# Expert stage of a two-layer encoder: evictions queued one chunk behind their matmuls, one-hots two chunks ahead, splits of 2048 columns with four chunks of room and seven raw buffers

## The chip, the cores and the metric

One core of a Trainium2 chip runs the whole kernel. The metric is device time in microseconds (us), taken as the median of several runs. The profile is one execution, recorded by the hardware profiler; its engines are PE (TensorE matmuls; PEld are its weight loads), DVE (VectorE), ACT (ScalarE), POOL (GpSimd) and SP (SyncE, which here issues the weight loads from HBM).

## What is computed

Two layers of a post-norm encoder trunk on 256 tokens of width 1024. Layer 1 ends in a dense SwiGLU, layer 2 in a top-2-of-8 expert SwiGLU:

```
logits = x @ w_router + b_router
gates  = softmax over the top 2 of 8, zero elsewhere
out    = sum over e of gates[:, e] * ((silu(x @ w1[e]) * (x @ w3[e])) @ w2[e])
x      = LayerNorm(alpha * x + out + ple)
```

Each expert has w1 and w3 of 1024 x 3584 and w2 of 3584 x 1024, all float32: 352 MB for the eight, and every byte is read once. The change touches only this expert stage, which in the kernel before runs from about 685 us to 1620 us of the span.

## The kernel before

**Accuracy scheme.** PE multiplies in float32r. To keep float32 accuracy, every operand is split in two: `hi` is the value rounded to float32r (a copy on ACT, line 95), `lo` is the value minus `hi` (a subtraction on DVE, line 96). A product then takes three matmuls: hi.hi, hi.lo, lo.hi (`mm3`, lines 253 to 255). So every weight that arrives is read once by ACT and once by DVE before PE can use it.

**Chunks.** The expert weights come as 336 chunks of 1 MB, each a tile of 128 x 2048 floats. SP loads chunk g into a raw buffer; there are nine, in the order of `MOE_RAW` (the tags misc, Q, Q, act, act, raw x4). `prepare` splits it as two halves of 1024 columns, each into one `hl` tile that holds hi and lo of the half; there is room for six halves (`MOE_HL`), that is for three chunks. `prepare` runs four halves ahead of the half that PE multiplies (`MOE_LEAD = 4`). A raw buffer is loaded again once the second half's subtraction has read it; a room is written again once PE has multiplied the half in it.

**Experts and blocks.** A routing step orders the experts by their number of tokens. The first four are *heavy* (128 slots), the last four *light* (64 slots, where hi and lo of the tokens lie side by side in the 128 columns, so that two matmuls do instead of three, lines 1216 and 1217). Each expert's 3584 hidden columns are cut in blocks of 1024, 1024, 1024 and 512. From the third block on, light and heavy blocks alternate. For block i the program goes through w1 (`kind` 0), half of the second multiplication (w2, `down`) of block i-1, w3 (`kind` 1), and the other half of that `down`: twelve chunks for a full block.

**Small work between chunks.** After a part, `gated` takes its results out of PSUM (silu or copy on ACT, a product on DVE). `turn` transposes the hidden block for `down`: eight transposes for a heavy block; for a light one 32 small matmuls against a folding matrix (line 1270), then for each of two tiles a silu on ACT (line 1273), a product on DVE (line 1274) and a split into `probT` (ACT, then DVE). `gather` picks an expert's tokens with one-hot matrices (line 1200; the one-hots are made on DVE, line 938), its results are split into `act` tiles. `close` ends an expert: it splits the sums, builds a one-hot, turns it, and adds four scattered results to the accumulator (lines 994 to 996). The pieces of `gather` and `close` are jobs; `step` runs one after each chunk.

**Order.** The whole stage is in a manually scheduled region: each engine executes its instructions in the order in which the program issues them. A job issues its matmuls and the ACT and DVE instructions that read their result in one go, so that ACT and DVE stand at them until PE has come there, with the splits of later chunks queued behind.

Of the kernel before, what the change touches and what calls it, by code (L numbers as in the profile page):

```python
# [15 lines left out]
OP = mybir.AluOpType  # L16
# [36 lines left out]
class Trunk:  # L53
# [764 lines left out]
    def route(self, r, N, PL, gate):  # L818
# [14 lines left out]
        self.ahead(2)  # L833
        pT = self.ps([S])
# [53 lines left out]
        for job in moe.gather(0):  # L888
            job()
# [202 lines left out]
class Experts:  # L1092
    def __init__(self, T):
# [19 lines left out]
        self.jobs, self.hots, self.xe, self.A, self.H, self.Y = [], {}, {}, {}, {}, {}  # L1113
# [66 lines left out]
    def gather(self, g):  # L1180
# [4 lines left out]
        def part(k0):  # L1185
# [16 lines left out]
            ks = slice(k0, k0 + per)  # L1202
            xe = self.xe[ps[0]]
            T.split(xe[:, 0, ks, :], xe[:, 1, ks, :], pt[:, :, :CAP])
            if len(ps) > 1:
                two = self.xe[g, "two"]
                T.split(two[:, :, ks, :LIGHT], two[:, :, ks, LIGHT:],
                        pt[:, :, CAP:].rearrange("p k (l c) -> p l k c", l=2))
# [12 lines left out]
    def up(self, i, kind, c, j, P):  # L1221
        p, b = self.blocks[i]
        hi, lo = self.hl[2 * self.at[i, kind, c] + j]
        xe, n = self.xe[p], hi.shape[1]
        for k in range(n):
            kk = n * (2 * c + j) + k
# [5 lines left out]
    def down(self, i, c, j):  # L1232
        p, b = self.blocks[i]
        hi, lo = self.hl[2 * self.at[i, 2, c] + j]
        if b == 0 and c == 0 and j == 0:
            self.Y[p] = [self.T.ps([512], "accB" if self.light(p) else "accA") for _ in range(2)]
        n = self.width(i) // 128
        kk = 2 * c + j
        h = self.H[i][kk // 4]
        two = h[:, kk % 4, :] if self.light(p) else (h[0][:, kk % 4, :], h[1][:, kk % 4, :])  # L1240
        for m in range(2):
            f = slice(512 * m, 512 * (m + 1))
            self.mul(self.Y[p][m], p, two, hi[:, 0, f], lo[:, 0, f],
                     b == 0 and kk == 0, b == len(BLOCKS) - 1 and kk == n - 1)
# [16 lines left out]
    def turn(self, i):  # L1261
        T, nc = self.T, self.nc
        self.H[i] = []
        cols = lambda t: t.rearrange("m (c p k) -> m c k p", c=2, k=2)
        if self.light(self.blocks[i][0]):
            for a, b in zip(self.A.pop((i, 0)), self.A.pop((i, 1))):
# [5 lines left out]
                s = T.shape(a[:, :4 * LIGHT], [4, LIGHT])  # L1272
                nc.scalar.activation(s, pt[:, 0], AF.Silu)
                nc.vector.tensor_tensor(s, s, pt[:, 1], op=OP.mult)
                h = T.s2k([4, CAP], F32R, "probT")
                T.split(h[:, :, :LIGHT], h[:, :, LIGHT:], s)
                self.H[i].append(h)
        else:
            for s in self.A.pop((i, 0)):
# [3 lines left out]
                h = T.s2k([4, CAP], F32R, "probT"), T.s2k([4, CAP], F32R, "probT")  # L1283
                T.split(*h, pt)
                self.H[i].append(h)

    def close(self, p):
        T, r = self.T, self.r
        yy = T.scatter_split(self.Y.pop(p))
        tiles = {}  # L1290
# [7 lines left out]
        def turned():  # L1298
            tiles["hotT"] = hotT = T.s2k([S], F32R)
            T.hot_transposed(hotT, tiles["hot"].rearrange("p t a b -> p t (a b)"))  # L1300

        def add(tb, j):
            T.scatter(yy[j], tiles["hotT"], r["gate_at"][:, tb, p:p + 1], self.acc, tb, j)

        self.jobs += [hot, turned]
        self.jobs += [lambda tb=tb, j=j: add(tb, j) for tb in range(2) for j in range(2)]

    def step(self):
        if self.jobs:
            self.jobs.pop(0)()  # L1310
# [179 lines left out]
```

## Time and profile before

| | |
|---|---|
| median of 3 runs | 1638.17 us (1637.68 to 1638.29) |
| profiled execution | 1638.37 us, span 1636.5 us |
| PE busy, whole span | 1570.8 us (96%) |
| DVE busy, whole span | 1362.4 us (83%) |
| ACT busy, whole span | 1136.0 us (69%) |
| DMA | 469.91 MB, mean 287 GB/s |

The profiled execution's time is 1.9 us more than its span, and 0.2 us from the median. The shares are means over the whole span; the expert stage has other ones. A busy PE here is not PE at its peak, since the ends of matmuls are modelled. Times in the rows further down are us from the start of the span, unless marked ns.

### The profile page before, as it was taken

The page shows a single profiled execution, that of the slowest core. Times are in us where ns is not written, and L with a number is a line of the kernel's source. Part 1 is how long each engine was busy: PE and PEld are TensorE (multiplying, and loading weights), DVE is VectorE, ACT ScalarE, POOL GpSimd, SP SyncE. Part 2 cuts the span into 40 slices and gives each one's busy share as a digit, 9 for nine tenths or more (in the row PEclk, how much of TensorE's full clock was granted, in tenths as well). Part 3 has the DMA queues.
Part 4 walks back from the last instruction along what each step waited for, and adds up shares of the span by engine and source line. Part 5 has one row for each costly group of instructions (what it writes and reads, how often), then busy time and mean ns, then how long its engine had stood idle before and what let it go on. Part 6 is the DMA issues. An engine that isn't in the chain of part 4 may idle for free. (4 is left out here: it accounts for less than half of the span.)

```text
span 1636.5 us, 24338 instructions
## 1 busy us (share of the span) xinstructions
PE 1570.8 (96%) x8969; PEld 1324.1 (81%) x8969; DVE 1362.4 (83%) x1687; ACT 1136.0 (69%) x1557; POOL 66.3 (4%) x113
## 2 busy tenths in 40 slices
PE   8999999999999999989999999999999999999995
PEld 7999989999899998867876777777778777777763
DVE  5797766555668877889999999889999899999996
ACT  4577555444547765658888887788788788887883
POOL 3310000000021000000000000000000000000000
PEclk9999999999999999999999999999999999999997
DMA  8364655565542757579999999989999999999990
GB/s 288 93 183 134 238 174 187 181 191 193 178 131 62 222 201 259 177 262 370 408 407 410 387 408 358 374 338 406 388 400 361 351 393 394 401 375 391 405 381 27
DMA packets 164990, 469.91 MB, mean 287 GB/s; under 512 B 10121, under 2 KB 68561, under 8 KB 150529
## 3 DMA queue, kind: packets, MB, share of 16 engines
q1 hardware_dynamic: 162400, 462.19, 76.0%
q0 software_dynamic: 2176, 5.58, 1.3%
q8 instruction: 72, 1.18, 0.3%
q10 hardware_dynamic: 288, 0.52, 0.1%
q14 instruction: 54, 0.43, 0.1%
HBM read 467.21 MB, written 1.05 MB: 286 GB/s over the span
## 5 line engine op out<-in xcount | busy, mean ns | idle before, releaser
L96 DVE TENSOR_TENSOR hl<-raw,hl 128x1024 fp32r<-128x1024 f32 (+2 forms) x430 | 496.5, 1184 | 132.9 <-ACT hl L95 132.4
L95 ACT CAST hl<-raw 128x1024 fp32r<-128x1024 f32 (+2 forms) x430 | 426.3, 1022 | 181.1 <-PE mm L255 118.4
L253 PE MATMUL mm<-act,hl 128*128 128x256 f32 x1080 | 306.6, 284 | 0.4 <-ACT hl L95 0.4
L255 PE MATMUL mm<-act,hl 128*128 128x256 f32 x1080 | 306.6, 284 | 0.0
L254 PE MATMUL mm<-act,hl 128*128 128x256 f32 x1080 | 305.9, 283 | 0.0
L253 PEld LDWEIGHTS mm<-act,hl 128*128 128x128 f32 x1080 | 207.1, 192 | 2.2 <-ACT hl L95 0.8
L254 PEld LDWEIGHTS mm<-act,hl 128*128 128x128 f32 x1080 | 207.1, 192 | 0.8
L255 PEld LDWEIGHTS mm<-act,hl 128*128 128x128 f32 x1080 | 207.1, 192 | 0.4
L96 DVE TENSOR_TENSOR hl<-Q,hl 128x1024 fp32r<-128x1024 f32 x152 | 177.3, 1217 | 6.8 <-ACT hl L95 6.3
L95 ACT CAST hl<-Q 128x1024 fp32r<-128x1024 f32 x152 | 152.0, 1054 | 6.1 <-PE mm L255 4.4
L1217 PE MATMUL mm<-hl,act 128*64 128x512 f32 x304 | 122.7, 411 | 6.7 <-DVE hl L96 6.7
L1216 PE MATMUL mm<-hl,act 128*128 128x512 f32 x304 | 123.1, 405 | 0.8 <-ACT hl L95 0.8
L254 PE MATMUL mm<-hl,act 128*128 128x512 f32 x304 | 118.7, 390 | 2.6 <-DVE hl L96 2.6
L253 PE MATMUL mm<-hl,act 128*128 128x512 f32 x304 | 119.0, 392 | 1.6 <-DVE act L96 1.6
L255 PE MATMUL mm<-hl,act 128*128 128x512 f32 x304 | 118.4, 390 | 0.0
L96 DVE TENSOR_TENSOR K<-raw,K 128x1024 fp32r<-128x1024 f32 x78 | 91.8, 1216 | 0.7 <-ACT K L95 0.7
L96 DVE TENSOR_TENSOR K<-misc,K 128x1024 fp32r<-128x1024 f32 x76 | 89.5, 1216 | 1.2 <-ACT K L95 1.1
L96 DVE TENSOR_TENSOR hl<-act,hl 128x1024 fp32r<-128x1024 f32 x74 | 87.1, 1216 | 1.2 <-ACT hl L95 1.2
L96 DVE TENSOR_TENSOR K<-act,K 128x1024 fp32r<-128x1024 f32 x74 | 87.0, 1216 | 0.6 <-ACT K L95 0.5
L95 ACT CAST K<-raw 128x1024 fp32r<-128x1024 f32 x78 | 78.7, 1051 | 2.7 <-PE mm L255 1.7
L1216 PEld LDWEIGHTS mm<-hl,act 128*128 128x128 f32 x304 | 59.1, 194 | 24.2 <-ACT hl L95 1.9
L95 ACT CAST K<-misc 128x1024 fp32r<-128x1024 f32 x76 | 76.6, 1053 | 2.7 <-PE mm L255 2.3
(360 smaller groups left out, 3194.1 us busy)
## 6 DMA issues: line engine op xcount, KB each, us to landing
raw<-in_moe_w_dram SPq DMA_DIRECT2D x148, 1024.0 KB, 7.8
Q<-in_moe_w_dram SPq DMA_DIRECT2D x76, 1024.0 KB, 8.1
act<-in_moe_w_dram SPq DMA_DIRECT2D x74, 1024.0 KB, 10.8
misc<-in_moe_w_dram SPq DMA_DIRECT2D x38, 1024.0 KB, 7.9
raw<-in_w_in_dram SPq DMA_DIRECT2D x35, 1024.0 KB, 5.3
raw<-in_ffn_w_dram SPq DMA_DIRECT2D x33, 1024.0 KB, 5.3
raw<-in_w_out_dram SPq DMA_DIRECT2D x8, 1024.0 KB, 6.2
raw<-in_w_ple_gate_dram SPq DMA_DIRECT2D x8, 1024.0 KB, 5.0
```

Of the source, the lines that this page charges most:

```text
L95: self.nc.scalar.copy(hi, src)
L96: self.nc.vector.tensor_tensor(lo, src, hi.bitcast(F32), op=OP.subtract)
L253: mm(out, ah, bh, start=first, stop=False)
L254: mm(out, ah, bl, start=False, stop=False)
L255: mm(out, al, bh, start=False, stop=last)
L1216: full = lambda: mm(out, two, hi, start=first, stop=last)
L1217: half = lambda: mm(out[:LIGHT], two[:, :LIGHT], lo, start=False, stop=False)
```

## The change

- **Splits of 2048 columns.** `prepare` splits a whole chunk at once: one copy on ACT and one subtraction on DVE per chunk, 336 of each in place of 672. hi and lo get a tile of 2048 columns each.
- **Four chunks of room, seven raw buffers.** The room tags are now K, Q and hl twice, each with two tiles; the two Q tiles are no longer raw buffers. `prepare` runs three chunks ahead of PE.
- **Evictions a chunk behind.** `turn`, `gather` and the adds of `close` now return a function with their ACT and DVE instructions. `step` keeps it in `pending` and issues it after the next chunk's split and matmuls. `gated` and `close` go through `pending` too.
- **One-hots two chunks ahead.** The jobs of a gather are the one-hot, an empty one, then the matmuls. For `close`, the one-hot and its transpose (`hot_jobs`) are queued at the start of the expert's last block.
- **Order of the jobs.** The one-hot and gather of the second group go ahead of the jobs that are waiting (`ple_sum`), and one chunk is split before the router's matmuls.

```diff
-MOE_RAW = ["misc", "Q", "Q", "act", "act", "raw", "raw", "raw", "raw"]
-MOE_HL = ["K", "K", "hl", "hl", "hl", "hl"]
-MOE_LEAD = 4
+MOE_RAW = ["misc", "act", "act", "raw", "raw", "raw", "raw"]
+MOE_HL = ["K", "Q", "hl", "hl"]
+MOE_LEAD = 3
...
+        moe.prepare(1)
         pT = self.ps([S])
...
     def prepare(self, upto):
-        while len(self.hl) < min(upto, 2 * len(self.chunks)):
-            q = len(self.hl)
-            g, j = q // 2, q % 2
+        T = self.T
+        while len(self.hl) < min(upto, len(self.chunks)):
+            g = len(self.hl)
             self.fetch(g + 1)
-            self.hl.append(self.T.halve(self.raws[g], j, 2, "k", MOE_HL[q % len(MOE_HL)]))
-            if j == 1:
-                self.fetch(g + 1 + len(MOE_RAW))
+            raw = self.raws[g]
+            tag = MOE_HL[g % len(MOE_HL)]
+            hl = [T.act(list(raw.shape[1:]), F32R, tag=tag) for _ in range(2)]
+            T.split(*hl, raw)
+            self.hl.append(hl)
+            self.fetch(g + 1 + len(MOE_RAW))
...
     def turn(self, i):
...
-                s = T.shape(a[:, :4 * LIGHT], [4, LIGHT])
-                nc.scalar.activation(s, pt[:, 0], AF.Silu)
-                nc.vector.tensor_tensor(s, s, pt[:, 1], op=OP.mult)
-                h = T.s2k([4, CAP], F32R, "probT")
-                T.split(h[:, :, :LIGHT], h[:, :, LIGHT:], s)
-                self.H[i].append(h)
+                todo.append((pt, T.shape(a[:, :4 * LIGHT], [4, LIGHT])))
...
+        def out():
+            for pt, s in todo:
+                if s is None:
+                    h = T.s2k([4, CAP], F32R, "probT"), T.s2k([4, CAP], F32R, "probT")
+                    T.split(*h, pt)
+                else:
+                    nc.scalar.activation(s, pt[:, 0], AF.Silu)
+                    nc.vector.tensor_tensor(s, s, pt[:, 1], op=OP.mult)
+                    h = T.s2k([4, CAP], F32R, "probT")
+                    T.split(h[:, :, :LIGHT], h[:, :, LIGHT:], s)
                 self.H[i].append(h)
...
+    def settle(self):
+        todo, self.pending = self.pending, []
+        for out in todo:
+            out()
+
+    def step(self, job=None):
+        self.settle()
+        if job is None and self.jobs:
+            job = self.jobs.pop(0)
+        out = job and job()
+        if out:
+            self.pending.append(out)
...
-                self.jobs += [lambda g=g: self.hot(g)] + self.gather(g)
+                jobs = [lambda g=g: self.hot(g), lambda: None] + self.gather(g)
+                self.jobs = jobs + self.jobs
+            if i < n and self.blocks[i][1] == len(BLOCKS) - 1:
+                self.jobs += self.hot_jobs(self.blocks[i][0])
...
                 if kind < 2:
-                    self.gated(b, kind, P)
+                    self.pending.append(lambda b=b, kind=kind, P=P: self.gated(b, kind, P))
```

What stands where is decided by this order. Three places follow. In the names, `raw`, `misc`, `act` and `Q` behind the arrow are raw buffers, `K`, `Q` and `hl` ahead of it are rooms; `prob` and `mm` are a light block's hidden values and the PSUM banks of its fold.

On DVE, at the first `turn` of a light block, the kernel before has these rows:

```order
L96 TENSOR_TENSOR hl_1165_8261<-raw_1132_8099,hl_1165_8261 128x1024
L96 TENSOR_TENSOR hl_1166_8270<-raw_1132_8099,hl_1166_8270 128x1024
L1274 TENSOR_TENSOR prob_1133_8105<-prob_1133_8105,mm_1168_8281 128x256
L96 TENSOR_TENSOR probT_1169_8292<-prob_1133_8105,probT_1169_8292 128x4x64
L1274 TENSOR_TENSOR prob_1134_8106<-prob_1134_8106,mm_1170_8295 128x256
L96 TENSOR_TENSOR probT_1171_8306<-prob_1134_8106,probT_1171_8306 128x4x64
L96 TENSOR_TENSOR hl_1172_8309<-raw_1137_8121,hl_1172_8309 128x1024
```

On DVE, at the same `turn`, the changed kernel has these:

```order
L96 TENSOR_TENSOR hl_1167_8196<-misc_1141_8081,hl_1166_8195 128x2048
L96 TENSOR_TENSOR K_1172_8232<-act_1146_8101,K_1171_8231 128x2048
L1298 TENSOR_TENSOR prob_1137_8073<-prob_1137_8073,mm_1169_8213 128x256
L96 TENSOR_TENSOR probT_1174_8251<-prob_1137_8073,probT_1174_8251 128x4x64
L1298 TENSOR_TENSOR prob_1138_8074<-prob_1138_8074,mm_1170_8222 128x256
L96 TENSOR_TENSOR probT_1175_8256<-prob_1138_8074,probT_1175_8256 128x4x64
L96 TENSOR_TENSOR Q_1177_8260<-act_1149_8115,Q_1176_8259 128x2048
```

The four short rows keep their order among themselves; they now stand one chunk's split later relative to PE's fold, between two splits of 2048 columns.

On ACT, at the same place, the kernel before has these rows:

```order
L95 CAST hl_1166_8270<-raw_1132_8099 128x1024
L1273 ACTIVATE prob_1133_8105<-mm_1168_8281 128x256
L95 CAST probT_1169_8292<-prob_1133_8105 128x4x64
L1273 ACTIVATE prob_1134_8106<-mm_1170_8295 128x256
L95 CAST probT_1171_8306<-prob_1134_8106 128x4x64
L95 CAST hl_1172_8309<-raw_1137_8121 128x1024
L95 CAST hl_1173_8318<-raw_1137_8121 128x1024
```

On ACT, the changed kernel has these there:

```order
L95 CAST K_1171_8231<-act_1146_8101 128x2048
L1297 ACTIVATE prob_1137_8073<-mm_1169_8213 128x256
L95 CAST probT_1174_8251<-prob_1137_8073 128x4x64
L1297 ACTIVATE prob_1138_8074<-mm_1170_8222 128x256
L95 CAST probT_1175_8256<-prob_1138_8074 128x4x64
L95 CAST Q_1176_8259<-act_1149_8115 128x2048
```

The copy that follows the four is one of 2048 columns, where a half of 1024 stood.

On DVE, at the gather of the third group, the kernel before makes the one-hots one job ahead of their use (`iota`), and the gathered results go into `act`:

```order
L938 TENSOR_SCALAR s2k_1587_10413<-iota_6904,s1_at_7405 128x64 x4
L96 TENSOR_TENSOR K_1588_10420<-raw_1552_10239,K_1588_10420 128x1024
L96 TENSOR_TENSOR K_1589_10427<-raw_1552_10239,K_1589_10427 128x1024
L96 TENSOR_TENSOR act_1591_10436<-mm_1593_10438,act_1591_10436 128x256
L96 TENSOR_TENSOR act_1592_10437<-mm_1593_10438,act_1592_10437 128x2x2x64
L96 TENSOR_TENSOR hl_1594_10451<-raw_1557_10259,hl_1594_10451 128x1024
```

On DVE, the changed kernel has three splits there:

```order
L939 TENSOR_SCALAR s2k_1588_10151<-iota_6904,s1_at_7405 128x64 x4
L96 TENSOR_TENSOR Q_1590_10159<-misc_1561_10023,Q_1589_10158 128x2048
L96 TENSOR_TENSOR hl_1593_10173<-act_1564_10041,hl_1592_10172 128x2048
L96 TENSOR_TENSOR hl_1599_10198<-act_1567_10059,hl_1598_10197 128x2048
L96 TENSOR_TENSOR act_1595_10186<-mm_1597_10188,act_1595_10186 128x256
L96 TENSOR_TENSOR act_1596_10187<-mm_1597_10188,act_1596_10187 128x2x2x64
L96 TENSOR_TENSOR K_1605_10233<-raw_1570_10077,K_1604_10232 128x2048
```

Between the one-hots and the first use of the gathered result there are now three chunks' splits instead of one.

## Rows read from the trace of the kernel before

**Rows 1.** Windows: busy us (and instructions) per engine, PEclk, DMA share, GB/s.

```profile
687.00:1609.00 922.00, 882.39 (x4067) 679.98 (x4065) 868.73 (x882) 745.44 (x877) 0.00 (x0) 0.99 0.96 373
800.00:900.00 100.00, 97.83 (x451) 72.69 (x450) 96.43 (x94) 84.52 (x100) 0.00 (x0) 1.00 1.02 408
1000.00:1100.00 100.00, 94.70 (x454) 74.56 (x453) 88.48 (x96) 77.37 (x97) 0.00 (x0) 0.98 0.93 354
```

**Rows 2.** Timeline of DVE, stage's first and last splits: start, us, what.

```profile
687.75 4.63 DVE L96 TENSOR_TENSOR hl<-Q,hl 128x1024 fp32r<-128x1024 f32 x4 [0.25 <-ACT hl L95]
...
1606.71 2.35 DVE L96 TENSOR_TENSOR hl<-Q,hl 128x1024 fp32r<-128x1024 f32 x2
```

**Rows 3.** Waits of DVE, 700 to 1600 us: total, times, longest.

```profile
DVE hl L96 <- ACT hl L95: 17.2, 29, 1.5
DVE probT L96 <- ACT probT L95: 13.4, 28, 0.6
DVE prob L1274 <- ACT prob L1273: 11.4, 19, 1.0
```

**Rows 4.** Groups by form, 700 to 1600 us: busy us, mean ns.

```profile
L96 DVE TENSOR_TENSOR hl<-raw,hl 128x1024 fp32r<-128x1024 f32 x222 | 259.6, 1216 | 10.1 <-ACT hl L95 9.9
L96 DVE TENSOR_TENSOR probT<-prob,probT 128x256 fp32r<-128x256 f32 x27 | 11.5, 425 | 12.7 <-ACT probT L95 12.7
...
L95 ACT CAST hl<-act 128x1024 fp32r<-128x1024 f32 x72 | 73.1, 1054 | 3.2 <-PE accA L255 1.7 <-PE mm L255 0.9 <-DVE K L96 0.3
L95 ACT CAST probT<-prob 128x256 fp32r<-128x256 f32 x27 | 11.0, 406 | 19.1 <-DVE prob L1274 19.1
```

**Rows 5.** Timeline of DVE, the smallest split.

```profile
660.47 0.21 DVE L96 TENSOR_TENSOR s2k<-s2k,s2k 128x64 fp32r<-128x64 f32 x1
```

**Rows 6.** Timeline of DVE at a light turn.

```profile
1085.15 0.42 DVE L1274 TENSOR_TENSOR prob<-prob,mm 128x256 f32<-128x256 f32 x1 [1.01 <-ACT prob L1273]
...
1087.04 0.42 DVE L1274 TENSOR_TENSOR prob<-prob,mm 128x256 f32<-128x256 f32 x1 [0.57 <-ACT prob L1273]
1087.93 0.43 DVE L96 TENSOR_TENSOR probT<-prob,probT 128x256 fp32r<-128x256 f32 x1 [0.47 <-ACT probT L95]
1088.88 2.36 DVE L96 TENSOR_TENSOR hl<-raw,hl 128x1024 fp32r<-128x1024 f32 x2 [0.53 <-ACT hl L95]
```

**Rows 7.** Timeline of ACT at the same turn.

```profile
1084.74 0.38 ACT L1273 ACTIVATE prob<-mm 128x256 f32<-128x256 f32 x1 [3.32 <-PE mm L1270]
1087.81 1.99 ACT L95 CAST hl<-raw 128x1024 fp32r<-128x1024 f32 x2
```

**Rows 8.** Timeline of DVE at gathers: the third group's, then the last group's.

```profile
1054.95 2.36 DVE L96 TENSOR_TENSOR hl<-raw,hl 128x1024 fp32r<-128x1024 f32 x2 [0.53 <-ACT hl L95]
...
1288.38 0.69 DVE L96 TENSOR_TENSOR act<-mm,act 128x512 fp32r<-128x512 f32 x1 [1.66 <-ACT act L95]
1293.87 0.69 DVE L96 TENSOR_TENSOR act<-mm,act 128x512 fp32r<-128x512 f32 x1 [2.18 <-ACT act L95]
```

**Rows 9.** Timeline of SP, two loads into misc, then landing times of all expert loads.

```profile
721.79 0.34 SPq L169 DMA_DIRECT2D misc<-in_moe_w_dram  x1
...
1576.81 0.35 SPq L169 DMA_DIRECT2D misc<-in_moe_w_dram  x1
...
DMA to landing us min/median/max: 4.8/8.2/15.4
```

**Rows 10.** Timeline of PE: a late one-hot, then 36 matmuls up to a fold.

```profile
1050.95 1.20 PE L1200 MATMUL mm<-s2k,act 128*128 128x256 f32 x8 [3.01 <-DVE s2k L938]
...
1074.53 0.39 PE L253 MATMUL accA<-K,probT 128*128 128x512 f32 x1
...
1082.72 1.04 PE L1270 MATMUL mm<-fold,prob 128*128 128x64 f32 x8
```

**Rows 11.** Timeline of PE at the end of the stage.

```profile
1610.34 0.79 PE L1216 MATMUL accB<-hl,probT 128*128 128x512 f32 x1 [4.28 <-DVE probT L96]
...
1619.55 0.79 PE L994 MATMUL mm<-s2k,s2k 128*128 128x512 f32 x1 [0.46 <-ACT s2k L1002]
```

More of the change, by code (lines that the diff above doesn't have):

```diff
@@ L1201, in part @@
                         m += 1
[L1202 to L1208, printed above, removed]
+            def out():
+                ks = slice(k0, k0 + per)
+                xe = self.xe[ps[0]]
+                T.split(xe[:, 0, ks, :], xe[:, 1, ks, :], pt[:, :, :CAP])
+                if len(ps) > 1:
+                    two = self.xe[g, "two"]
+                    T.split(two[:, :, ks, :LIGHT], two[:, :, ks, LIGHT:],
+                            pt[:, :, CAP:].rearrange("p k (l c) -> p l k c", l=2))
+            return out
         return [lambda k0=k0: part(k0) for k0 in range(0, KT, per)]
@@ L1298, in turned, with out, close @@
         def turned():
-            tiles["hotT"] = hotT = T.s2k([S], F32R)
-            T.hot_transposed(hotT, tiles["hot"].rearrange("p t a b -> p t (a b)"))
-        def add(tb, j):
-            T.scatter(yy[j], tiles["hotT"], r["gate_at"][:, tb, p:p + 1], self.acc, tb, j)
-        self.jobs += [hot, turned]
-        self.jobs += [lambda tb=tb, j=j: add(tb, j) for tb in range(2) for j in range(2)]
-    def step(self):
-        if self.jobs:
-            self.jobs.pop(0)()
+            hot = tiles.pop("hot").rearrange("p t a b -> p t (a b)")
+            pt = T.ps([2, 128])
+            for tb in range(2):
+                self.nc.tensor.transpose(pt[:, tb, :], hot[:, tb, :].bitcast(F32), T.ident)
+            def out():
+                tiles["hotT"] = hotT = T.s2k([S], F32R)
+                self.nc.scalar.copy(hotT, pt.rearrange("p t c -> p (t c)"))
+            return out
+        return [hot, lambda: None, turned]
+    def close(self, p):
+        T, r = self.T, self.r
+        yy = T.scatter_split(self.Y.pop(p))
+        def add(tb, j):
+            hotT = self.spread[p]["hotT"]
+            t = slice(tb * 128, (tb + 1) * 128)
+            pt = T.ps([512])
+            self.nc.tensor.matmul(pt, hotT[:, t], yy[j][0], start=True, stop=False)
+            self.nc.tensor.matmul(pt, hotT[:, t], yy[j][1], start=False, stop=True)
+            def out():
+                c = slice(512 * j, 512 * (j + 1))
+                self.nc.vector.scalar_tensor_tensor(self.acc[:, tb, c], pt, r["gate_at"][:, tb, p:p + 1],
+                                                    self.acc[:, tb, c], op0=OP.mult, op1=OP.add)
+            return out
+        self.jobs += [lambda: None]
+        self.jobs += [lambda tb=tb, j=j: add(tb, j) for tb in range(2) for j in range(2)]
+    def settle(self):
[9 more added lines that the diff above has]
+            self.pending.append(out)
     def flush(self):
@@ L1314, in flush @@
             self.step()
+        self.settle()
     def run(self):
@@ L1345, in run @@
                 if b == len(BLOCKS) - 1:
-                    self.close(p)
+                    self.pending.append(lambda p=p: self.close(p))
+        self.settle()
 class Gate:
```

59 lines of the change are left out of this document (31 added, 28 removed).

## Prediction, made before the changed kernel ran

> **What bounds the kernel now.** The change lies in the expert stage, so the first view is the table of windows over that stage alone. From 687 to 1609 us DVE is busy for 868.7 of 922 us, PE for 882.4, ACT for 745.4, and the DMA engines move 373 GB/s [rows 1]. Three candidates are close, and the shares do not decide among them. PE's share is inflated, since modelled ends of matmuls overlap. The DMA reaches 408 GB/s in one stretch of 100 us and falls to 354 in another [rows 1], so it is not held at a ceiling throughout.
>
> The second view decides: the waits of DVE. Its idle time is 922 - 869 = 53 us, and the largest entries are all waits for ACT: 17.2 us at a weight's subtraction for its own copy, 13.4 at `probT`, 11.4 at the product of `turn` [rows 3]. Nothing in DVE's queue waits for a load. DVE works or stands in step with ACT from the first split at 687.75 to the end of the last at 1609 [rows 2], and PE and SP follow it. So the stage costs what DVE's queue costs, and I add up that queue.
>
> How much room do the others have? PE: 36 back-to-back matmuls take 1082.72 - 1074.53 = 8.19 us [rows 10], 0.2275 each. The stage has 168 heavy chunks of 12 and 168 light ones of 8, 3360 x 0.2275 = 764 us. 448 folds at no more than 1.04/8 = 0.13 [rows 10] add 58, the 112 transposes and 96 gather matmuls at the same price 27, the 64 scattered ones 15: 864 of 922 us, 58 us of room. The loads: misc is every ninth, so from the 19th at 721.79 to the 334th at 1576.81 [rows 9] a chunk takes 855/315 = 2.714 us. At the 408 GB/s of [rows 1], 1.0486 MB takes 2.570 us. Over 315 chunks this is 45 us of room.
>
> **The change, part by part (DVE's queue).**
>
> *Splits of 2048 columns.* Four halves back to back take 4.63 us, and one by itself 1.216 [rows 2, 4], so they start (4.63 - 1.216)/3 = 1.138 us apart: an instruction overlaps the next by 0.078, and a chunk costs 2.276. No row has 2048 columns. From 256 and 1024 columns (425 and 1216 ns) [rows 4] a column is 1.030 ns, and the chunk 1.216 + 1.055 = 2.271, less the overlap 2.193: 0.083 saved. From 64 columns (0.21 us) [rows 5] a column is 1.048 ns, the chunk 2.289 - 0.078 = 2.211: 0.065 saved. Over 336 chunks this is 28 or 22 us; I take 24. The bounds are 0 (a chunk costs two halves) and the whole fixed part, 1.216 - 1024 x 0.00103 = 0.161, which would be 54.
>
> [...]
>
> *Evictions behind a split, at light turns.* Today ACT reaches the first silu 3.32 us before PE's fold is done [rows 7], and DVE waits 1.01 us there and 0.57 at the second [rows 6]. A chunk later the folds are done, so these waits go: 11.4 us in all [rows 3], about 10 of it won. The waits for the `probT` copies, 0.47 each [rows 6], stay: product, copy and subtraction still take turns. Bounds: 0 and 11.4.
>
> *The same at gathers.* In the last group DVE waits 1.66 and 2.18 us for a copy that waits for PE's gather [rows 8]. Both go, with about 3 us of smaller ones: 7 won. Bounds: 3 and 9.
>
> *What it costs.* ACT's last `probT` copy waits for DVE, and the next weight's copy is queued behind it. Today that copy is a half, and DVE waits 0.53 us for it [rows 6, 8]. A copy of 2048 columns takes 1.054 + 1024 x (1.054 - 0.406)/768 = 1.92 us [rows 4], 0.86 more than a half, and DVE cannot begin before its end. This happens after 15 light turns and 8 gather parts: 23 x 0.86 = 20 us given back. Bounds: 0, if ACT were ahead at these places, which its dependence on DVE's product excludes for the turns; 20 above. I take 20.
>
> *One-hots two chunks ahead.* They take away PE's waits, like the 3.01 us at 1050.95 [rows 10]. DVE does the same one-hots in either place, so by its queue this is 0; from 0 to 10 us, should PE's late matmuls hold DVE back further than its waits show.
>
> *Evictions later for PE.* A result now leaves PSUM after the next chunk's split, some 4 us later, and PE can stand at a bank or at `probT`, above all in the eight blocks of 512, where `down` follows two chunks after `turn`. At 4 us each this is 32 us at most, inside PE's 58; I take 0.
>
> *Four chunks of room, seven raws.* A raw buffer must be back in seven chunks instead of nine, at today's pace 7 x 2.714 = 19.0 us instead of 24.4. Landing takes 8.2 us in the median [rows 9], copy and subtraction 1.92 + 2.28 = 4.2 more, together 12.4. I take 0 here; the worst landing is a rival below.
>
> *Start and end.* One chunk is split before the router's chain, while DVE has gaps: up to 2.3 us, I take 1. At the end PE waits 4.28 us for DVE, and its scatter starts at 1619.55, after a one-hot, a transpose and a copy that are now done earlier [rows 11]: up to 5, I take 3.
>
> **Sum.** -24 - 10 - 7 + 20 - 1 - 3 = -25 us on the profiled execution's 1638.4, which stands 0.2 us from the median: 1613 us.
>
> **Rivals.**
>
> *The longer copies eat the gain* (0.15). If the overhead saved is nearer 15 than 24 and only half of PE's late waits go, then -15 - 8 + 20 - 2 = -5: 1633 us. For it: the bubbles are certain by the order on ACT, and the savings are small amounts. Against it: the subtraction's slope is fixed by three widths.
>
> *The loads become the bound from below* (0.15). If the fixed part of the subtraction goes entirely (-54), or ACT keeps ahead at the turns, then DVE is faster than the loads, and the 45 us of their room are the end of it: about 1595 us. For it: 408 GB/s already stands over 100 us at a time. Against it: [rows 2] show the overlap.
>
> *Seven raws are too few* (0.10): slower. The place is SP's queue, which may issue load g + 7 only when chunk g is subtracted. If loads take the longest landing seen, 15.4 us [rows 9], a buffer's turn is 15.4 + 4.2 = 19.6 us, 2.80 per chunk, 0.086 above now: +27 us over 315 chunks, with nothing of the savings left, 1665 us. It decides from a landing of 19.0 - 4.2 = 14.8 us. Against it: the median is 8.2. For it: landing grows with the loads in the queue, and two buffers are taken out of the ring. [...]
>
> **How the numbers follow.** The forecast has 0.60, its own range being 1604 to 1622. A difference of 0.2%, 3.3 us, is about what a measurement of this kernel can tell from no change. The range reaches down to the loads' bound, 1595, and up past the eaten gain to 1638; the slower rival and some 0.05 of tails stay outside. Faster by more than 0.2%: 0.60, 0.15, and 0.08 of the eaten gain, 0.83. Within 0.2%: 0.06. Slower: 0.11.
>
> **What would show it.** After the change, the subtraction of 2048 columns lasts 2.27 to 2.29 us, with starts 2.19 to 2.21 apart. The waits of DVE lose the product's entry (11.4 to about 1), and keep `probT` near 13; the entry of weights waiting for their copies grows from 17 to 35 or more, in gaps of about 1.4 us after light turns. PE has no wait for one-hots. Loads come every 2.63 us. I am wrong if DVE now waits for loads or for rooms (then the ring of buffers is the bound), if its idle time falls well under 45 us (ACT keeps ahead), or if PE's waits for PSUM and `probT` reach its 58 us.

## The result, and the profile after

The changed kernel takes 1649.5 us in the median of 4 runs (1647.8 to 1650.8), the kernel before 1638.2: a ratio of 1.0069, interval 1.0051 to 1.0086. It is 11.3 us slower, where the prediction said 25 us faster. The profiled execution has a span of 1648.6 us against 1636.5.

Windows over the stage and two stretches of it, after, with the columns of [rows 1]:

```profile
687.00:1620.00 933.00, 887.24 (x4079) 690.66 (x4078) 845.93 (x553) 716.18 (x544) 0.00 (x0) 0.98 0.95 369
800.00:900.00 100.00, 99.40 (x454) 74.95 (x454) 94.02 (x57) 83.08 (x61) 0.00 (x0) 1.00 1.02 409
1000.00:1100.00 100.00, 94.33 (x434) 74.48 (x432) 87.53 (x62) 73.37 (x59) 0.00 (x0) 0.95 0.93 351
```

DVE has become 868.7 - 845.9 = 23 us cheaper, as forecast, and the stage is longer all the same: DVE's idle time went from 53 to 87 us. The groups by form say that the durations were right as well (ahead of the first bar the shape and count, behind it busy us and mean ns):

```profile
L96 DVE TENSOR_TENSOR Q<-raw,Q 128x2048 fp32r<-128x2048 f32 x48 | 109.8, 2286 | 14.1 <-ACT Q L95 13.9
L95 ACT CAST K<-act 128x2048 fp32r<-128x2048 f32 x24 | 45.9, 1912 | 29.1 <-PE accA L254 16.7 <-PE mm L254 10.5 <-ACT hl L95 1.8
```

The waits (700 to 1600 us: total, times, longest) show what DVE stands for. Of DVE, to be read against [rows 3], then of ACT, then of PE:

```profile
DVE Q L96 <- ACT Q L95: 25.6, 31, 1.8
DVE K L96 <- ACT K L95: 18.8, 16, 7.3
DVE hl L96 <- ACT hl L95: 18.4, 24, 1.4
DVE probT L96 <- ACT probT L95: 11.8, 25, 0.5
...
ACT hl L95 <- PE mm L254: 18.9, 24, 0.8
ACT K L95 <- PE accA L254: 18.8, 10, 5.8
ACT Q L95 <- PE mm L254: 18.4, 21, 3.3
...
PE accA L255 <- DVE probT L96: 11.0, 3, 3.7
PE mm L1288 <- DVE prob L1269: 9.3, 4, 6.3
PE mm L1337 <- DVE probT L96: 5.2, 3, 1.8
PE mm L253 <- ACT prob L1266: 4.6, 1, 4.6
```

Read as a ring: DVE waits for its own copies (62.8 us at the three room tags), ACT's copies wait for PE to free a room (line 254 is the last matmul that reads `lo`), and PE waits for small results that stand in DVE's queue. The product's entry (11.4 us in [rows 3]) is gone.

**Where the time went.** The blocks are the same in both kernels, so their lengths can be compared: a block ends with the last subtraction of its last chunk on DVE. Worked out so from the timelines of DVE, in us against the kernel before (the first column is layer 1 and what else lies ahead of the stage, whose code is unchanged; "start" is blocks 0 and 1; "short" is the three light blocks of 512 columns that lie between others, and the blocks behind them; "gathers" is the two later blocks with a gather; then the other blocks, 84, 32 and 112 chunks; the last chunks; and what follows the last subtraction):

| version (experiment) | ahead of it | start | short | gathers | heavy 1024 | heavy 512 | light | last | tail | span |
|---|---|---|---|---|---|---|---|---|---|---|
| changed | +3.5 | +6.5 | +13.0 | +0.3 | -3.7 | -2.6 | -3.8 | -2.6 | +1.3 | +12.1 |
| all at once (1) | +1.4 | +3.3 | +5.1 | -2.4 | -4.1 | -0.5 | -8.0 | -0.1 | -1.4 | -6.7 |
| turn at once (2) | +3.6 | +6.7 | +2.5 | +0.3 | -4.6 | +0.8 | -4.8 | -2.5 | +0.5 | +2.6 |
| three rooms (3) | +2.9 | +7.1 | +15.4 | -1.4 | +11.4 | +3.9 | -0.4 | -1.8 | +0.9 | +38.1 |
| jobs as before (4) | 0.0 | +4.4 | +13.6 | +0.3 | -3.7 | -2.6 | -4.5 | -2.5 | +1.6 | +6.6 |
| halves (5) | +1.9 | +1.3 | +9.7 | -5.4 | -5.3 | -4.8 | -0.6 | -2.3 | +0.8 | -4.7 |
| whole splits alone (6) | +0.3 | +4.8 | +1.2 | +3.0 | +1.9 | -2.1 | -2.7 | 0.0 | +3.6 | +9.9 |
| two ahead (7) | +0.4 | +0.9 | +3.4 | -3.4 | -4.0 | -0.1 | -8.0 | -2.1 | +0.6 | -12.3 |
| pairs (8) | +0.6 | -3.9 | +4.3 | -7.6 | -8.3 | +6.7 | -0.8 | -2.6 | -0.9 | -12.5 |
| one ahead (9) | +3.0 | +1.5 | +6.9 | -1.0 | +7.2 | +6.3 | -7.2 | +2.7 | -6.9 | +12.5 |
| pairs, two ahead (11) | +2.9 | -6.1 | +0.5 | -7.7 | -8.5 | -1.7 | -0.2 | -3.0 | -1.7 | -25.4 |
| once, two ahead (12) | +1.3 | +3.9 | +5.8 | -1.3 | +7.2 | +8.6 | -7.7 | +0.3 | -1.6 | +16.6 |

In the changed kernel 19.5 us are lost at the start and at three short blocks, and 12.7 won in the ordinary ones. 3.5 of its 12.1 us fall on unchanged code: each row is one execution, not all on one chip, and the first column, from 0 to 3.6, shows how far two of them differ by themselves.

**A short block.** The timelines of DVE, PE and ACT in the changed kernel, and two windows over PE's stall and what follows it (the granted clock is the third number from the end):

```profile
936.24 1.28 DVE L1269 TENSOR_TENSOR prob<-prob,mm 128x512 f32<-128x512 f32 x2
937.44 2.29 DVE L96 TENSOR_TENSOR K<-raw,K 128x2048 fp32r<-128x2048 f32 x1
939.64 2.28 DVE L96 TENSOR_TENSOR Q<-raw,Q 128x2048 fp32r<-128x2048 f32 x1
941.84 2.29 DVE L96 TENSOR_TENSOR hl<-raw,hl 128x2048 fp32r<-128x2048 f32 x1
944.04 1.28 DVE L96 TENSOR_TENSOR probT<-mm,probT 128x512 fp32r<-128x512 f32 x2
...
937.67 1.11 PE L1288 MATMUL mm<-ident,prob 128*128 128x128 f32 x8
944.78 0.80 PE L255 MATMUL accA<-K,probT 128*128 128x512 f32 x1 [3.68 <-DVE probT L96]
945.38 0.63 PE L253 MATMUL accA<-K,probT 128*128 128x512 f32 x1
948.67 0.40 PE L253 MATMUL accA<-Q,probT 128*128 128x512 f32 x1
...
939.45 1.06 ACT L95 CAST probT<-mm 128x512 fp32r<-128x512 f32 x2
...
948.64 1.91 ACT L95 CAST K<-act 128x2048 fp32r<-128x2048 f32 x1 [5.81 <-PE accA L254]
950.59 2.29 DVE L96 TENSOR_TENSOR K<-act,K 128x2048 fp32r<-128x2048 f32 x1 [2.67 <-ACT K L95]
...
941.00:944.70 3.70, 0.10 (x1) 0.00 (x0) 3.70 (x4) 1.83 (x2) 0.00 (x0) 0.98 1.02 404
945.00:948.40 3.40, 3.40 (x9) 2.68 (x10) 2.92 (x4) 0.00 (x0) 0.00 (x0) 0.56 1.02 408
```

PE has turned the hidden block by 938.8, and its copies are made, but three whole chunks stand in DVE's queue ahead of `probT`. PE waits 3.68 us, frees no room meanwhile, so ACT waits 5.81 and DVE 2.67. In the kernel before the wait at this place is 0.97 us:

```profile
933.56 0.50 PE L255 MATMUL accA<-hl,probT 128*128 128x512 f32 x1 [0.97 <-DVE probT L96]
```

Behind the long wait ten matmuls take 948.67 - 944.78 = 3.89 us instead of 10 x 0.2275. That is 2.7 us of stall more and 1.6 of slow clock: 4.3 a place, and 13.0/3 = 4.3 in the table.

**The start.** PE, ACT and DVE in the changed kernel:

```profile
711.86 0.79 PE L253 MATMUL mm<-K,act 128*128 128x512 f32 x1 [4.61 <-ACT prob L1266]
735.16 1.98 PE L1288 MATMUL mm<-ident,prob 128*128 128x128 f32 x8 [6.28 <-DVE prob L1269]
...
704.66 0.37 ACT L95 CAST act<-mm 128x256 fp32r<-128x256 f32 x1 [4.72 <-DVE act L96]
709.53 0.37 ACT L95 CAST act<-mm 128x256 fp32r<-128x256 f32 x1 [2.42 <-DVE act L96]
711.21 1.08 ACT L1266 ACTIVATE prob<-mm 128x512 f32<-128x512 f32 x2
...
717.62 2.29 DVE L96 TENSOR_TENSOR K<-act,K 128x2048 fp32r<-128x2048 f32 x1 [7.27 <-ACT K L95]
```

Here the silu that frees PE's PSUM bank stands on ACT behind two gather copies, each of which waits for a subtraction that stands on DVE behind whole chunks.

### The profile page after: what moved, and what is told of

Same layout as the page of the kernel before. It is cut to its first block, busy times and chain, and to the rows that moved or that the text cites. A ratio compares the mean times of both kernels' runs of the same rounds, so it can differ in the third digit from the quotient of the medians.

```text
span 1648.6 us, 23362 instructions
## 1 busy us (share of the span) xinstructions
PE 1575.2 (96%) x8969; PEld 1335.1 (81%) x8969; DVE 1342.1 (81%) x1351; ACT 1106.8 (67%) x1221; POOL 65.0 (4%) x113
## 5 line engine op out<-in xcount | busy, mean ns | idle before, releaser
L96 DVE TENSOR_TENSOR hl<-raw,hl 128x1024 fp32r<-128x1024 f32 (+3 forms) x304 | 454.6, 1509 | 130.7 <-ACT hl L95 128.7
L95 ACT CAST hl<-raw 128x1024 fp32r<-128x1024 f32 (+3 forms) x304 | 385.2, 1281 | 192.9 <-PE mm L255 110.8
L96 DVE TENSOR_TENSOR Q<-raw,Q 128x2048 fp32r<-128x2048 f32 (+1 forms) x52 | 114.5, 2205 | 16.6 <-ACT Q L95 16.5
L96 DVE TENSOR_TENSOR K<-raw,K 128x2048 fp32r<-128x2048 f32 (+1 forms) x52 | 114.6, 2205 | 6.7 <-ACT K L95 4.1
L96 DVE TENSOR_TENSOR hl<-act,hl 128x2048 fp32r<-128x2048 f32 x48 | 109.3, 2286 | 11.7 <-ACT hl L95 11.7
L95 ACT CAST Q<-raw 128x2048 fp32r<-128x2048 f32 (+1 forms) x52 | 95.9, 1847 | 22.1 <-PE mm L254 9.6
L95 ACT CAST K<-raw 128x2048 fp32r<-128x2048 f32 (+1 forms) x52 | 95.9, 1846 | 9.8 <-PE mm L254 6.3
L1225 PE MATMUL mm<-hl,act 128*128 128x512 f32 x256 | 101.6, 397 | 0.0
L95 ACT CAST hl<-act 128x2048 fp32r<-128x2048 f32 x48 | 91.3, 1914 | 12.2 <-PE mm L254 8.8
L253 PE MATMUL mm<-hl,act 128*128 128x512 f32 x192 | 75.3, 392 | 0.0
L255 PE MATMUL mm<-hl,act 128*128 128x512 f32 x192 | 74.8, 390 | 0.0
L254 PE MATMUL mm<-hl,act 128*128 128x512 f32 x192 | 74.8, 389 | 0.0
L96 DVE TENSOR_TENSOR K<-act,K 128x2048 fp32r<-128x2048 f32 x24 | 54.9, 2288 | 15.7 <-ACT K L95 15.6
```

What stands on the lines that cost most here:

```text
L95: self.nc.scalar.copy(hi, src)
L96: self.nc.vector.tensor_tensor(lo, src, hi.bitcast(F32), op=OP.subtract)
L253: mm(out, ah, bh, start=first, stop=False)
L254: mm(out, ah, bl, start=False, stop=False)
L255: mm(out, al, bh, start=False, stop=last)
L1225: full = lambda: mm(out, two, hi, start=first, stop=last)
```

## The experiments

Theory 1: the loss is the place of the evictions in the queues of ACT and DVE. Theory 2: it is the buffers, whole-chunk rooms and seven raws. An eviction is deferred if it is issued a chunk behind its matmuls, as in the changed kernel, and at once if it is issued right behind them, as before. The lead is the number of chunks split ahead of PE. Ratios are to the kernel before on the same chip, with 95% intervals; the changed kernel's is 1.0069.

**1. Nothing deferred.**

```diff
         out = job and job()
         if out:
-            self.pending.append(out)
+            out()
...
-                    self.pending.append(lambda b=b, kind=kind, P=P: self.gated(b, kind, P))
+                    self.gated(b, kind, P)
...
-                    self.pending.append(lambda p=p: self.close(p))
+                    self.close(p)
```

> The changed kernel with no eviction deferred: `step` issues a job's evictions right behind its matmuls, and `gated` and `close` run at once; splits of 2048 columns, four rooms, seven raws and early one-hots stay. Block by block, the changed kernel loses 13.9 us in block 1, and 3.2 and 1.1 us at each of the three places where a block of 512 columns begins (13 us together), and gains 14.5 us in all the other blocks. Theory 1 (the evictions come too late for PE at these places): the 13 us come back, most of the 13.9 too, and the waits at light turns and gathers return (10 + 7): 1649.5 - 13 - 11 + 14 = about 1640, with the short blocks at 20.6 us again. Theory 2 (whole-chunk rooms and seven raws eat the gain, and the late evictions only show where): no more than 3 us come back, 1646 to 1660.

1631.0 us, ratio 0.997 (0.9958 to 0.9982): faster than both kernels. The short blocks come down by 8, the start only by 3, and light blocks gain 4 more. I had expected 1640: the 17 us that the returning waits at light turns and gathers were to cost did not come. DVE's wait at the product is back with 5.4 us, and the heavy blocks of 1024 are no longer than in the changed kernel (229.4 us against 229.8). Theory 1 stands, but not all of the start is deferral.

**2. Only `turn` at once.**

```diff
                         self.step(lambda: self.turn(i - 1))
+                        self.settle()
```

> The changed kernel with the evictions of `turn` alone issued right behind its matmuls; gathers, gated results and adds stay a chunk behind. Theory 1: the three short blocks go from 23.8 back to about 20.6 us and those behind them by 1.1 (13 us won), and light turns lose part of the 10 us that deferral had won there: 1649.5 - 13 + 5 = 1641 (1636 to 1646). Theory 2: within 3 us of 1649.5, or slower.

1638.3 us, ratio 1.0016 (1.0007 to 1.0026). The short group falls from +13.0 to +2.5 and nothing else moves by more than 3.4: the stall at these places comes from the deferred `turn` (PE's wait there is 1.48 us instead of 3.68).

**3. Three rooms, nine raws.**

```diff
-MOE_RAW = ["misc", "act", "act", "raw", "raw", "raw", "raw"]
-MOE_HL = ["K", "Q", "hl", "hl"]
-MOE_LEAD = 3
+MOE_RAW = ["misc", "Q", "Q", "act", "act", "raw", "raw", "raw", "raw"]
+MOE_HL = ["K", "hl", "hl"]
+MOE_LEAD = 2
```

> The changed kernel with three whole-chunk rooms (K, hl, hl), two chunks ahead, and nine raw buffers (the two Q tiles are raws again). Theory 1 (late evictions): where PE stands for probT little changes, 1646 to 1655. Theory 2 with the rooms as the bound: a room less makes DVE wait more for its copies, 1660 or more. Theory 2 with the raws as the bound (in the changed kernel a chunk's copy begins as little as 0.1 us after its landing in seven blocks, where before the least was 5): faster than 1645.

1674.2 us, ratio 1.0233 (1.0219 to 1.0248). It is 27 us slower than the changed kernel, 15 of them in heavy blocks of 1024, and two more raws make up for nothing. The waits of ACT here, then of DVE:

```profile
ACT hl L95 <- PE mm L254: 53.4, 62, 3.4
ACT hl L95 <- PE accA L254: 38.5, 31, 4.5
...
DVE hl L96 <- ACT hl L95: 54.0, 87, 7.2
```

So with three rooms the rooms bound the heavy stretches. Against experiment 7, which has the same lead, four rooms and two raws less, this is 2.9%, 48 us. No run changes the raws alone.

**4. Jobs in the order of before.**

```diff
-                jobs = [lambda g=g: self.hot(g), lambda: None] + self.gather(g)
-                self.jobs = jobs + self.jobs
+                self.jobs += [lambda g=g: self.hot(g), lambda: None] + self.gather(g)
```

> The changed kernel with the jobs in the order of before: `ple_sum` first, then the one-hot and the gather of the second group. Only blocks 0 and 1 can change. Theory 1a (at the start the gather, brought forward, stands between the weight copies and the silu of block 0, and PE waits 4.6 us for that silu and 6.3 us for the product): block 1 goes from 52.4 back to about 40 us, the whole to about 1638. Theory 1b (the deferral of silu and product is the cause, whatever the order of the jobs): block 1 stays at 50 or more, the whole within 3 us of 1649.5.

1645.1 us, ratio 1.0058 (1.0044 to 1.0072). Only 2 of the 6.5 us at the start come back. Block 1 takes 45.8 us, between the two theories. PE's waits for the silu and the product (4.6 and 6.3 us) are gone, as 1a has it, but 6.9 us of waits for `act` subtractions and 2.4 for a one-hot stand in their place.

**5. Halves.** `prepare`, `up` and `down` as before, with six rooms of halves, four halves ahead and nine raws; deferral, one-hots and order as changed.

```diff
-MOE_RAW = ["misc", "act", "act", "raw", "raw", "raw", "raw"]
-MOE_HL = ["K", "Q", "hl", "hl"]
-MOE_LEAD = 3
+MOE_RAW = ["misc", "Q", "Q", "act", "act", "raw", "raw", "raw", "raw"]
+MOE_HL = ["K", "K", "hl", "hl", "hl", "hl"]
+MOE_LEAD = 4
...
```

> The changed kernel with its splits as before: halves of 1024 columns, six rooms of halves, four halves ahead, nine raws; deferred evictions, early one-hots and the order of the jobs stay as changed. Theory 1 (a deferred eviction stands in DVE's queue behind the weights already split ahead, three chunks of 2.2 us; with four halves ahead behind two): the loss at the three short blocks shrinks from 13 us to some 6, the gather's bubbles go back to 0.53, the splits cost 0.07 us more per chunk wherever DVE is the bound: between the kernel before and the changed one, +3 to +9 us against before. Theory 2 (whole-chunk rooms and seven raws are what costs): as fast as before or faster.

1633.8 us, ratio 0.9975 (0.9964 to 0.9987): less than expected at the short blocks (9.7 lost, not 6), more won elsewhere. It is faster than before, as Theory 2 had it and Theory 1 (3 to 9 us slower) had not; but the lead fell with the halves, from three chunks to two, and experiment 7 shows that whole splits with a lead of two are no slower.

**6. Whole splits alone, in the kernel before.** `prepare`, `up`, `down` and these constants as changed, all else as before.

```diff
-MOE_RAW = ["misc", "Q", "Q", "act", "act", "raw", "raw", "raw", "raw"]
-MOE_HL = ["K", "K", "hl", "hl", "hl", "hl"]
-MOE_LEAD = 4
+MOE_RAW = ["misc", "act", "act", "raw", "raw", "raw", "raw"]
+MOE_HL = ["K", "Q", "hl", "hl"]
+MOE_LEAD = 3
...
```

> The kernel before with the splits alone changed: whole chunks, four rooms, three chunks ahead, seven raws; evictions at once, one-hots and jobs as before. Theory 1 (the late evictions and the job order are the loss, the splits are the gain): short blocks at 20.6 us, block 1 within 3 us of 38.5, blocks of gathers 3 us longer by the longer bubbles, the others 0.3 to 0.9 us shorter each: 8 to 14 us faster than before. Theory 2 (the long queue of whole chunks is itself what makes every result late at the start): block 1 at 43 or more, and no faster than the version with everything at once, 2 to 5 us under before.

1648.1 us, ratio 1.0059 (1.004 to 1.0078): Theory 1 as I had put it is wrong here, the splits alone are no gain. PE's waits for one-hots, in the kernel before, in this one and in the first experiment:

```profile
PE mm L1001 <- DVE s2k L938: 10.4, 4, 2.7
PE mm L1200 <- DVE s2k L938: 9.0, 3, 3.6
...
PE mm L1001 <- DVE s2k L938: 15.6, 6, 3.5
PE mm L1203 <- DVE s2k L938: 12.7, 3, 6.7
...
PE mm L1205 <- DVE s2k L939: 2.3, 2, 1.5
```

A one-hot issued just ahead of its matmuls makes PE wait 19.4 us in all with halves, and 28.3 with three whole chunks ahead. The first experiment differs by the earlier one-hots, the order and the first chunk, and is 0.9% faster; which of the three did how much of it, no run shows.

**7. Two chunks ahead.**

```diff
-MOE_LEAD = 3
+MOE_LEAD = 2
```

> The changed kernel with one constant changed: two chunks split ahead in place of three; four rooms, deferral and all else stay. Theory 1 with the depth of DVE's queue as the size of each stall (an eviction waits behind the chunks split ahead): the stall at each short block falls from 3.2 to 1 us or less, block 1 from 52 to 47 or less, 10 us or more faster than the changed kernel. Rival (the depth is needed to carry DVE over the heavy stretches): heavy blocks 1 to 2.5 us longer each, as with three rooms, 15 us or more slower than the changed kernel.

1627.5 us, ratio 0.9939 (0.9921 to 0.9956): one constant is worth 21 us. The short group falls to +3.4, the start to +0.9, gathers to -3.4. PE's wait at the place shown above, in this kernel (930 to 950 us):

```profile
PE accA L255 <- DVE probT L96: 2.1, 1, 2.1
```

**8. Pairs.** Copies of a pair ahead of its subtractions, heavy turns at once, light turns in two steps, block 0 at once, jobs as in 4.

```diff
+    def splits(self, parts):
+        for hi, lo, src in parts:
+            self.nc.scalar.copy(hi, src)
+        for hi, lo, src in parts:
+            self.nc.vector.tensor_tensor(lo, src, hi.bitcast(F32), op=OP.subtract)
...
+        def light():
+            for pt, s in todo:
+                nc.scalar.activation(s, pt[:, 0], AF.Silu)
+            for pt, s in todo:
+                nc.vector.tensor_tensor(s, s, pt[:, 1], op=OP.mult)
+            return turned
...
         for out in todo:
-            out()
+            more = out()
+            if more:
+                self.pending.append(more)
...
+                        if not self.light(self.blocks[i - 1][0]) or len(cs) == 2:
+                            self.settle()
...
```

> A candidate. The changed kernel with the turns of heavy blocks at once; light turns in two steps (both silus and products, a chunk later both copies and both subtractions); at gathers both copies ahead of both subtractions; silu and product of block 0 at once; jobs in the order of before. Theory 1: short blocks at 20.6 us (13 won, of which 9 showed with the turns alone at once); the gathers' bubbles of 1.38 and 0.44 us go, since ACT's next weight copy no longer stands behind a copy that waits for DVE: block 12 from 42.3 to 36 us, block 1 from 52.4 to 42 or less: 25 us faster than the changed kernel, about 14 faster than before. Theory 2 (rooms and raws): what is won at these places is lost by waits for rooms or loads in the blocks behind them, and the whole is within 5 us of before.

1627.3 us, ratio 0.9945 (0.9925 to 0.9965), 20 to 22 us under the changed kernel instead of the 25 expected. Heavy blocks of 512 lose 6.7. There (`len(cs) == 2`) the first step of a light turn is issued at once: ACT stands 2.85 and 1.50 us at the two silus for PE's folds, the next chunk's split comes behind them, `probT` behind that, and PE waits 2.13 us for it. In the changed kernel PE does not wait there, and 11 defers this step again.

**9. One chunk ahead.** `MOE_LEAD = 1`, else as changed.

> The changed kernel with one chunk split ahead in place of three, else unchanged. In an in-order queue a result that is evicted a chunk later stands where one evicted at once would stand with one chunk more ahead; so count the whole chunks queued ahead of an eviction: four in the changed kernel, three with two ahead or with everything at once (whose blocks agree within 0.5 us in all but a few), two here, and two in the kernel before. Theory 1 (this count sizes the stalls): block 1 and the gathers gain again, block 12 falls from 41.7 below 40, short blocks stay at 20.6; 4 to 10 us faster still than with two ahead, a ratio of 0.988 to 0.992. Rival (ACT and DVE now reach evictions before PE has done their matmuls, as they did before at light turns): heavy blocks 1 us or more longer each, a ratio above 0.996.

1650.6 us, ratio 1.008 (1.0066 to 1.0094): the rival came, and not the 0.988 to 0.992 of Theory 1. Waits of ACT and DVE, two ahead, then one:

```profile
ACT prob L1297 <- PE mm L1281: 43.2, 23, 3.2
DVE prob L1298 <- ACT prob L1297: 6.8, 13, 0.9
...
ACT prob L1297 <- PE mm L1281: 62.5, 25, 4.8
DVE prob L1298 <- ACT prob L1297: 25.0, 22, 1.8
```

Now ACT reaches a silu before PE has done the fold, DVE stands behind it, and heavy blocks of 1024 take 11 us more than in experiment 7, those of 512 another 6. What Theory 1 did say of the stalls holds: PE's wait for `probT` at the short blocks is gone.

**10. At once and one ahead.** The edit of 1 with `MOE_LEAD = 1`.

> Everything evicted at once and one chunk split ahead: one whole chunk queued ahead of an eviction. Theory 1 has its optimum where an eviction comes to its engine just behind PE; here ACT and DVE should come too early and stand for PE (11 us of such waits at light turns and 7 at gathers stood in the kernel before, with two ahead), with no stall of PE left to win against it: slower than with two chunks ahead of an eviction, by 5 to 20 us, a ratio of 0.993 to 1.005. Rival (the fewer ahead the better, all the way): a ratio below 0.988.

1865.5 us, ratio 1.1402 (1.138 to 1.1425). The direction was right, the size not: ACT alone stands 74 us for folds (line 1281) and 66 for transposes (line 1288), and with one chunk ahead PE then waits 127 us for DVE's splits.

**11. Pairs and two ahead.** Experiment 8 with these lines besides (`short` is set in blocks of 512):

```diff
-MOE_LEAD = 3
+MOE_LEAD = 2
...
-            return turned
+            return turned() if short else turned
...
-                        if not self.light(self.blocks[i - 1][0]) or len(cs) == 2:
+                        if not self.light(self.blocks[i - 1][0]):
```

> A candidate that joins what won: two chunks ahead; turns of heavy blocks at once; light turns in two steps, in blocks of 512 in one step a chunk behind; copies ahead of subtractions at gathers; silu and product of block 0 at once; jobs in the order of before. If the gains of the version with two ahead (21 us under the changed kernel) and of the candidate with three ahead (20 us) lie at different places, as their blocks say (block 1: 38 us with the pairs, 42 with two ahead; block 12: 36 against 42; the blocks (1,0), (2,0), (3,0): 1.3 us better each with the pairs; blocks of 512 after light ones 1 to 3 better without), they add up to some 15 us more: a ratio of 0.982 to 0.988. Theory 2 (loads): with the stalls gone the loads are late, since chunks are already copied 0.1 us after landing in six blocks: no better than 0.992, with ACT waiting 10 us or more for DMA.

1612.7 us, ratio 0.9851 (0.9838 to 0.9865), 24 us faster than before. At the gathers of the third group DVE's gaps are gone behind all parts but the first, where 2.02 us are left; the changed kernel first, then this one (here a pair's two subtractions are one row):

```profile
1081.72 0.42 DVE L96 TENSOR_TENSOR act<-mm,act 128x256 fp32r<-128x256 f32 x1 [0.44 <-ACT act L95]
1083.53 2.29 DVE L96 TENSOR_TENSOR hl<-raw,hl 128x2048 fp32r<-128x2048 f32 x1 [1.38 <-ACT hl L95]
...
1060.54 0.75 DVE L102 TENSOR_TENSOR act<-mm,act 128x256 fp32r<-128x256 f32 x2
1061.21 2.28 DVE L96 TENSOR_TENSOR Q<-raw,Q 128x2048 fp32r<-128x2048 f32 x1
```

ACT's and DVE's waits in this kernel name no load: the loads are not yet the bound.

**12. At once and two ahead.** The edit of 1 with `MOE_LEAD = 2`.

> Everything evicted at once, two chunks ahead: two whole chunks queued ahead of an eviction, as in the deferred version with one ahead (1650.6 us, ratio 1.008). Theory 1 (only the count of chunks ahead of an eviction matters, not whether it comes from the lead or from the deferral): the same as that version, a ratio of 1.004 to 1.012, with ACT waiting some 60 us at light turns' silus for PE's folds. Rival (the deferral is of use by itself, since it puts a weight copy between a matmul and its eviction whatever the lead): no more than 5 us from the deferred version with two ahead, a ratio of 0.992 to 0.998.

1654.9 us, ratio 1.011 (1.0093 to 1.0127), as Theory 1 said, with 62.0 us of ACT's waits at the silus.

**What follows from them together.** Count the whole chunks whose splits are issued ahead of an eviction and behind that of the chunk just multiplied: the lead, and one more if it is deferred by a chunk. (At the short block above one of the four was done when PE came there; three stood in the queue.) With four rooms and early one-hots the ratios are: four (changed): 1.0069. Three: 0.997 at once, 0.9939 deferred. Two: 1.011 at once, 1.008 deferred. One: 1.14. In the ordinary blocks a chunk of deferral and a chunk of lead do the same: with three, heavy blocks of 1024 take 229.4 us at once and 229.5 deferred, light ones 279.9 and 279.9; with two 240.7 and 240.7, and 280.2 and 280.7. Three is best, and the change went past it because it raised both. PE's wait at the short blocks grows with the count: none with two whole chunks (experiments 9, 11 and 12), 0.97 us with two chunks in halves (before), 1.0 to 2.3 with three (1.0 in 6, 1.48 in 2 and 8, 2.1 in 1 and 7, 2.3 with three rooms), 3.7 with four.

A rival is the spare room: three ahead fill all four rooms, two leave one free. ACT's waits for line 254, the rooms, are 95.9 us in the changed kernel and 61.1 in experiment 7. But experiment 1 fills all the rooms as well, and has 61.9; so these waits go with the count too. No run has a fifth room.

DVE and ACT keep the order of issue in the trace of the changed kernel: the two copies of the `probT` above are made from 939.45 to 940.51, but its subtractions start at 944.04, behind three whole chunks, and PE stands 3.68 us for them; and the silu of block 0 runs at 711.21, behind gather copies that waited 4.72 and 2.42 us.

In ratios, the change can be walked in three steps: deferral, one-hots and order with halves, -0.25% (experiment 5); whole splits with their rooms and raws and the same three chunks ahead, -0.36% (5 to 7); the fourth chunk ahead, +1.30% (7 to the changed kernel). The last outweighs the others.

## Why the prediction was wrong

**The step that failed** is *Evictions later for PE*: "some 4 us later ... inside PE's 58; I take 0". The delay was sized about right (two more chunks of 2.2 us in the queue; PE waits 2.7 us longer at the short blocks). That it would be covered was wrong, in three ways. While PE stands, no room comes free, and ACT and DVE stop with it (5.81 and 2.67 us at the one shown), so that its idle time is no reserve. The stall of 3.68 us cost clock besides (0.56 in the 3.4 us behind it). And the places were not the eight blocks of 512: it was three of them (13.0 us) and the start (6.5), where the silu and the product of block 0 come late. My bound of 32 us was large enough; the 0 was not. *Four chunks of room* took 0 as well and looked at loads alone: the lead that goes with the rooms, two chunks to three, is half of this delay, and I did not name it.

**"The stage costs what DVE's queue costs"** holds only in some blocks. Windows over a heavy block (expert 0, its third) and a light one (expert 7, its second), of the kernel before and then of the changed one:

```profile
782.23:814.39 32.16, 32.16 (x158) 26.68 (x157) 29.12 (x30) 25.18 (x30) 0.00 (x0) 1.00 1.02 407
1503.07:1532.72 29.65, 28.51 (x125) 20.03 (x124) 29.65 (x30) 27.24 (x32) 0.00 (x0) 1.00 1.02 405
...
791.41:823.18 31.77, 31.77 (x156) 26.44 (x156) 28.30 (x17) 23.71 (x19) 0.00 (x0) 1.00 1.02 412
1517.94:1547.52 29.58, 29.28 (x127) 20.59 (x127) 29.00 (x17) 27.19 (x20) 0.00 (x0) 1.00 1.01 399
```

In the heavy block PE has no idle time; DVE got 0.8 us cheaper there and the block 0.4 shorter. In the light block of the kernel before it is DVE that has none. PE's 58 us of room and DVE's 53 idle were means over both kinds.

**Splits, -24.** Right as a duration (2286 ns; starts 939.64 - 937.44 = 2.20 apart) and as DVE's busy time (-23). As time it is right where DVE is the bound: from halves to wholes at three chunks ahead of an eviction (experiments 5 and 7, which differ in rooms and raws as well) the light blocks gain 7.4 us in 112 chunks, 0.066 each, against the forecast's 0.065 to 0.083. Elsewhere some of it is lost again, which leaves -0.36% or 5.9 us in all.

**Late waits at light turns, -10.** The entry went, as said. Light turns lie in heavy blocks, though, where PE sets the time: those of 1024 gained 3.7 us with everything in, and 4.1 in experiment 1, where half of the entry is back. So the term was worth nothing there. **Gathers, -7, and bubbles, +20.** The bubble is 1.38 us, as forecast. At gathers the two together came to +0.3, near what was priced: block 12 is 3.4 us longer, 4 x 0.86, and block 20, where the waits of 1.66 and 2.18 us [rows 8] stood, 3.0 shorter. At light turns the bubble costs less than 0.86: without it (experiment 8) the seven heavy blocks of 1024 are 4.6 us shorter than in the changed kernel, 0.66 each, and with the shorter one of the halves (5) 1.3 us shorter than in 7, 0.19 each.

**One-hots, 0.** Undersized: late one-hots made PE wait 19.4 us before and 28.3 with whole chunks ahead, and without early ones the splits are no gain (experiment 6 against 1, 15 us, with the order and the first chunk in it). Not all of these waits went: 3.4 us are left in the changed kernel, where none was forecast. **Start, -1, and tail, -3.** +6.5, and +1.3: the early one-hots gave 5.0 at the end (6 to 1), the deferred results took 2.7 of it (1 to the changed kernel), and the whole splits 3.6 before that (6).

**The rivals.** Seven raws were not it: ACT's waits for loads are 3.4 us in the changed kernel, and experiment 7 is faster than before with the same seven. But the gaps of DVE name ACT, ACT's name PE, which frees a room, and a room less costs 48 us. I had read the gaps one step back alone, where they name no load. What the prediction says of landing holds: in the trace of the kernel before it takes 5.2 us in the median with one other transfer under way at the issue, 8.9 with three and 13.4 with five. Of the signs listed for being wrong one came, the waits for rooms. PE's waits for PSUM and `probT` came to some 21 us (11.0, 5.2 and 4.6 in the list above; 26 with two smaller entries behind `act`), far from the 58, and the kernel is slower all the same.

What stays open: why three deferred is 0.3% better than three at once (by the table at the start, the short blocks and the last chunks), why with halves PE waits 3.5 us at each short block, though three chunks stand ahead there too, why experiment 6 has only 1.0 there, and how the loss at the start divides between order and deferral (experiments 1, 4 and 7 bring back 3.2, 2.1 and 5.6 of its 6.5 us).

## What to carry to other kernels

In the queues of this kernel the lead of a prefetch and the deferral of an eviction acted much like one number (with three chunks the heavy blocks of 1024 take 229.4 us at once and 229.5 deferred): how much stands ahead of a small result that another engine waits for. Count it before and after a change, and measure one step to either side; here one constant was worth 1.3%. Add up the queue of each engine for each kind of block: from experiment 5 to 7 the whole splits came with 7.4 us won in the light blocks, and with 1.3 lost in the heavy ones of 1024. And do not take the mean idle time of one engine (PE's 58 us here) as cover when it hands back the buffers of the others.

## What the chip showed that I had not expected

PE's clock was lower behind a single stall. Behind the wait of 3.68 us the granted clock over the next 3.4 us is 0.56 on the mean (0.57 and 0.68 behind the same wait at the other two short blocks): matmuls 0.43 us apart from 945.38 to 947.94, at a granted clock of 0.50, and from 948.67 on 0.23 apart, at 1.00; behind the 0.97 us at the same place before, the window shows 1.00:

```profile
933.60:936.50 2.90, 2.90 (x13) 2.40 (x14) 2.90 (x4) 2.86 (x4) 0.00 (x0) 1.00 1.01 388
```

So a stall of 2.7 us more cost 4.3.
